# A two-layer decoder segment on one core: second weight chunk in halves, the first norm's squares behind the first weight group, the first group read unscaled, the third group's chunks by parts

## The chip, the core and the metric

The kernel runs on one core of a Trainium2 chip. The metric is the device time of one execution in microseconds (us), as a median of several runs. The engines that matter are TensorE (PE, matrix products), ScalarE (ACT), VectorE (DVE), GpSimd (POOL, nearly idle here) and SyncE (SP), which issues nearly all DMA transfers. Each engine works through its own list of instructions in order; a PE product starts when its operands are there and the product ahead of it has made room.

## What is computed

The program is a decoder segment of two layers over 256 tokens of width 2048: an HGRN2 layer with 16 heads of 128, then a differential-attention layer, each followed by an MLP of width 8192 and a gated embedding. All weights are float32. The change touches only the beginning, the first norm and the first projections of the HGRN2 layer:

```python
def rms_norm(x, gain):
    y = x * rsqrt(mean(x * x, axis=-1) + EPS)
    return y * gain

h = rms_norm(x, ln_mix[0])
q_a, f_a, in_a, g_a = split(h @ a_w_in, 4)        # each (256, 16 heads x 128)
f = lb + (1 - lb) * sigmoid(f_a)                  # forget gate
o = hgrn2_chunkwise(silu(q_a), 1 - f, in_a, log(f))
o = rms_norm(o, a_onorm) * silu(g_a)
x = x + o @ a_w_out
...                                               # MLP, embedding, second layer
```

## The kernel before, in words

Every product of the projections is made in two parts, so that it has float32 accuracy: the weight W is split into a high part hi (a rounding of W) and a low part lo = W - hi, and so is the moving matrix xs. A weight group is 2048 x 512 values (four heads), read as eight chunks of 512 KB (2 x 128 rows by 512 columns) in order. `chunk` (L95 to L101) makes one: a load on SP's queue into `raw` (4 buffers), a cast of `raw` into `hi` on ACT (L99), and a subtraction into `lo` on DVE (L100); `hi` and `lo` have 3 buffers each. `first_chunk` (L103) does the same for the very first chunk in two halves of 256 KB, with its own cast (L113) and subtraction (L114).

`group_b` (L150) makes a group whose output has features on the partitions and tokens along the row. Its products are 128 x 128 of weight against 512 columns (`hi` against both parts of xs, L144) or 256 columns (`lo` against the high part, L147). Per chunk there are 8 pairs of one high and one low product; the sums of a group stay in two PSUM tiles (`mmps`), one for two of the four heads each. With `fresh=2` (group 1 alone) the first two chunks go by `mm_first` (L132, L135): all four heads' products of one half of a chunk before the next half, since xs is also still arriving. With `by_part`, a chunk's high products of a head come before its low ones; without it high and low alternate. The first chunks of the later groups go to the first PSUM tile alone and are caught up later (`for d in ...`), since the second tile may still be read.

At the end of a group `evac` in `project` (L537) reads the sums: for each of the two tiles ACT copies the low half into a buffer `t` (2 buffers, L545), DVE adds the two halves (L547) and, in the kernel before, multiplies by the norm's scale r (`RR[0]`, one value per token) into `z`. So the norm need not be known when the products start: xs is only x times the gain. `start` (L374) loads x transposed (`xa`, 8 pieces), makes xs from it (L200, L201), loads x in rows (`x`, four pieces of 512 KB) and forms the sums of squares of each piece: `square` (L209) writes the squares into a `t` buffer and their sum into `ss`, two ACT operations for each piece. `finish` (L234) then makes r = rsqrt(mean + eps), spreads it over the partitions by a product with a matrix of ones (L244) and copies it (L246).

The order of the groups is: forget gate of heads 0 to 3 (`do_f(0)`, weight group 4), their query (`do_q(0)`, group 0), forget gate of heads 4 to 7 (`do_f(1)`, group 5), their query (`do_q(1)`, group 1), and then the others. After the forget gate, `keys` (L556) turns z into k = 1 - f and G, the running sum of log f: absolute value, exp, log and exp on ACT (`sigmoid_steps`, L276 to L283), four affine operations (L566), a copy (L569), a log (L570), and four scans on DVE (L578, L580). After the query, `silu` does the same four ACT steps and a product on DVE. `hgrn` then computes the recurrence of four heads.

These side computations are Python generators: after each chunk of a group `pump` asks each of them for its next step, so their instructions are written between those of the chunks, and a scheduler orders each engine's list from that. A step written early waits in its engine's list, and whatever stands behind it there waits too. `z` has one buffer in `project` and one in `do_g`.

## Time and profile before

| | |
|---|---|
| median of 3 runs | 2505.16 us (2504.87 to 2505.43) |
| the profiled execution's own time | 2505.13 us |
| its span, first to last instruction in the trace | 2503.3 us |
| PE busy | 2496.0 us (100%) |
| DVE busy | 1544.5 us (62%) |
| ACT busy | 1305.4 us (52%) |
| DMA | 467 MB, 187 GB/s over the span |

The span is what the trace covers; 1.8 us lie around it. Busy time of PE includes products that overlap in its pipeline, so a row's duration in the timeline (0.39 us for a high product) is longer than the step from one product to the next (0.23 us for a high and 0.12 us for a low product). Where PE waited, the next product starts later than that step. Timeline rows of like instructions in a row are put together (x4); their duration is from the first's start to the last's end.

### The profile page before, as it was taken

To read this page: it belongs to the slowest core of one execution; us is meant where nothing else is said; L and a number is where in the kernel's file an instruction comes from. 1 tells how busy PE (TensorE), PEld (TensorE's weight loads), DVE (VectorE), ACT (ScalarE), POOL (GpSimd) and SP (SyncE) were. 2 spreads that over 40 slices of the span, in tenths; PEclk is the share of its full clock that TensorE was granted. 3 is DMA by queue.
4 is the path that set the end of the run, shared out by engine and by line. 5 is a ranking of instruction groups with operands and counts; after the bars stand their busy time and mean duration, and the time that the engine had idled before them with its cause. 6 is when DMAs were issued, how large, how long until landed. Compare 5 with 4: busy or idle time off the path is not lost.

```text
span 2503.3 us, 32238 instructions
## 1 busy us (share of the span) xinstructions
PE 2496.0 (100%) x12552; PEld 2114.3 (84%) x12552; DVE 1544.5 (62%) x1756; ACT 1305.4 (52%) x1669; POOL 6.1 (0%) x12
## 2 busy tenths in 40 slices
PE   9999999999999999999999999999999999999999
PEld 8888888888888888888888888888888888888887
DVE  7887886565565465565576576555556556555565
ACT  8666665444344444444576565544434434444455
POOL 0000000000000000000000000000000000000000
PEclk9999999999999999999999999999999999999999
DMA  7545455556555555555555545555556555555554
GB/s 275 185 152 184 158 172 180 185 186 193 193 188 192 194 192 191 189 193 187 190 179 186 185 151 173 168 185 186 193 189 194 191 193 190 196 192 188 188 201 158
DMA packets 130521, 466.99 MB, mean 187 GB/s; under 512 B 14528, under 2 KB 15168, under 8 KB 130368
## 3 DMA queue, kind: packets, MB, share of 16 engines
q1 hardware_dynamic: 130224, 464.93, 56.2%
q8 instruction: 98, 1.61, 0.3%
q14 instruction: 55, 0.45, 0.1%
q10 hardware_dynamic: 144, 0.01, 0.0%
HBM read 462.78 MB, written 2.10 MB: 186 GB/s over the span
## 4 chain that ended last, share of the span: by engine, by line
PE 99%; DMA 1%; DVE 0%; ACT 0%; SPq 0%; issue 0%
PE mmps L144 23%; PE mmps L175 20%; PE mmps L177 20%; PE mmps L176 20%; PE mmps L147 12%; PE smps L481 1%; PE smps L224 1%; DMA raw<-w_in 0%; DMA x<-x_r 0%; PE smps L512 0%; PE smps L444 0%; PE smps L783 0%; PE smps L819 0%; PE smps L847 0%; PE smps L818 0%; PE smps L530 0%
## 5 line engine op out<-in xcount | busy, mean ns | idle before, releaser
L100 DVE TENSOR_TENSOR lo<-raw,hi 128x1024 fp32r<-128x1024 f32 x869 | 1063.3, 1224 | 870.2 <-ACT hi L99 869.5
L99 ACT CAST hi<-raw 128x1024 fp32r<-128x1024 f32 x869 | 912.6, 1050 | 1045.5 <-PE mmps L177 618.1
L144 PE MATMUL mmps<-big,hi 128*128 128x512 f32 x2544 | 885.7, 395 | 0.0
L175 PE MATMUL mmps<-hi,big 128*128 128x512 f32 x2176 | 853.9, 392 | 0.0
L176 PE MATMUL mmps<-lo,big 128*128 128x512 f32 x2176 | 848.1, 390 | 0.0
L177 PE MATMUL mmps<-hi,big 128*128 128x512 f32 x2176 | 847.8, 390 | 0.0
L147 PE MATMUL mmps<-big,lo 128*128 128x256 f32 x2544 | 703.6, 278 | 0.3 <-DVE lo L100 0.3
L144 PEld LDWEIGHTS mmps<-big,hi 128*128 128x128 f32 x2544 | 476.3, 188 | 108.8
L177 PEld LDWEIGHTS mmps<-hi,big 128*128 128x128 f32 x2176 | 408.4, 188 | 86.0 <-DVE big L122 0.3
L147 PEld LDWEIGHTS mmps<-big,lo 128*128 128x128 f32 x2544 | 478.0, 188 | 3.0 <-DVE lo L100 1.2
L175 PEld LDWEIGHTS mmps<-hi,big 128*128 128x128 f32 x2176 | 408.6, 188 | 82.5
L176 PEld LDWEIGHTS mmps<-lo,big 128*128 128x128 f32 x2176 | 408.8, 188 | 82.1
L298 DVE SCALAR_TENSOR_TENSOR x<-mmps,r,x 128x512 f32<-128x512 f32 x64 | 45.2, 747 | 13.1 <-PE mmps L177 13.1
L200 ACT ACTIVATE big<-smps,sml 128x256 fp32r<-128x256 f32 x96 | 41.0, 471 | 18.0 <-DVE big L201 18.0
L122 DVE TENSOR_TENSOR big<-u,big 128x512 fp32r<-128x512 f32 x72 | 49.3, 685 | 0.0
L201 DVE SCALAR_TENSOR_TENSOR big<-smps,sml,big 128x256 fp32r<-128x256 f32 x96 | 42.2, 479 | 6.6 <-ACT big L200 6.0
L639 DVE SCALAR_TENSOR_TENSOR u<-u 128x512 f32<-128x512 f32 x64 | 44.3, 692 | 2.2
L121 ACT CAST big<-u 128x512 fp32r<-128x512 f32 x72 | 44.4, 616 | 1.9 <-DVE u L639 1.9
L289 ACT COPY t<-mmps 128x512 f32<-128x512 f32 x64 | 37.3, 583 | 14.5 <-PE mmps L147 14.5
L290 DVE TENSOR_TENSOR u<-mmps,t 128x512 f32<-128x512 f32 x64 | 43.8, 684 | 0.0
L212 ACT ACTIVATE t<-x 128x512 f32<-128x512 f32 x48 | 30.3, 631 | 3.9 <-DVE x L669 2.6
L467 ACT ACTIVATE E<-E 128x1024 f32<-128x1024 f32 x16 | 16.9, 1056 | 8.4 <-DVE E L466 8.2
(203 smaller groups left out, 905.2 us busy)
## 6 DMA issues: line engine op xcount, KB each, us to landing
raw<-w_up SPq DMA_DIRECT2D x256, 512.0 KB, 4.2
raw<-w_dn SPq DMA_DIRECT2D x256, 512.0 KB, 3.9
raw<-w_in SPq DMA_DIRECT2D x127, 512.0 KB, 3.3
raw<-w_pg SPq DMA_DIRECT2D x64, 512.0 KB, 3.4
raw<-w_ao SPq DMA_DIRECT2D x32, 512.0 KB, 3.2
raw<-w_k SPq DMA_DIRECT2D x32, 512.0 KB, 3.4
raw<-w_q SPq DMA_DIRECT2D x32, 512.0 KB, 3.3
raw<-w_v SPq DMA_DIRECT2D x32, 512.0 KB, 3.2
```

What stands on the lines that cost most here:

```text
L99: nc.scalar.copy(hi, raw)
L100: nc.vector.tensor_tensor(lo, raw, hi.bitcast(F32), ALU.subtract)
L121: nc.scalar.copy(dst[:, k, 0, :], src)
L122: nc.vector.tensor_tensor(dst[:, k, 1, :], src, dst[:, k, 0, :].bitcast(F32), ALU.subtract)
L144: nc.tensor.matmul(ps[:, ml, :], hi[:, k, w:w + P], rhs[:, k0 + k].rearrange("p a t -> p (a t)"), start=first and k == 0, stop=False)
L147: nc.tensor.matmul(ps[:, ml, T:2 * T], lo[:, k, w:w + P], rhs[:, k0 + k, 0, :], start=False, stop=last and k == KCS - 1)
L175: nc.tensor.matmul(out, xs[:, kc0 + k, 0, ts], hi[:, k], start=st, stop=False)
L176: nc.tensor.matmul(out, xs[:, kc0 + k, 0, ts], lo[:, k], start=False, stop=False)
L177: nc.tensor.matmul(out, xs[:, kc0 + k, 1, ts], hi[:, k], start=False, stop=en)
L290: nc.vector.tensor_tensor(out, ps[:, :, 0:T], t, ALU.add)
L298: nc.vector.scalar_tensor_tensor(xg, ps[:, tt], scale[:, tt, 0:1], xg, ALU.mult, ALU.add)
L639: nc.vector.scalar_tensor_tensor(u, u, 0.0, u, ALU.max, ALU.mult)
```

## The change

There are six edits, all of which act within the first 110 us or so:

- `first_chunk` becomes `fresh_chunk`, used for the first two chunks: chunk 2 of group 1 is now also loaded, cast and subtracted in halves.
- `start` runs over 13 steps in place of 8: the loads of x in rows go out at steps 6 to 9 (before: 4 to 7) and the squares of the four pieces at steps 9 to 12, which is behind group 1. The small constants are loaded one step later, the identity matrix at step 8.
- `finish` has one more step between the diagonal matrices and their product with ones.
- The first group is evacuated unscaled (`project(4 + j, j > 0)`): the sum of the halves is written straight to z. `keys(0)` waits until r is known and then multiplies z by it, in two DVE operations.
- `z` has two buffers in place of one.
- `by_part` is now a number of chunks: all eight for group 5 (the third group), three for group 1 (the fourth); in the MLP it stays at the first chunk.

```diff
@@ -100,19 +100,18 @@
         nc.vector.tensor_tensor(lo, raw, hi.bitcast(F32), ALU.subtract)
         return hi, lo
-    def first_chunk(src):
+    def fresh_chunk(src, c):
         raw = rp.tile([P, KCS, CW], F32, tag="raw", name="raw")
-        hi = wp.tile([P, KCS, CW], F32R, tag="hi", name="hi")
-        lo = wp.tile([P, KCS, CW], F32R, tag="lo", name="lo")
+        hi, lo = (wp.tile([P, KCS, CW], F32R, tag=n, name=n) for n in ("hi", "lo"))
         for k in range(KCS):
             nc.sync.dma_start(raw[:, k], src[:, k * CW:(k + 1) * CW])
-            if k == 0:
+            if c == k == 0:
                 load_xa(0)
         for k in range(KCS):
             nc.scalar.copy(hi[:, k], raw[:, k])
             nc.vector.tensor_tensor(lo[:, k], raw[:, k], hi[:, k].bitcast(F32), ALU.subtract)
-            if k == 0:
+            if c == k == 0:
                 gain_xa(0)
         return hi, lo
@@ -147,18 +146,18 @@
                     nc.tensor.matmul(ps[:, ml, T:2 * T], lo[:, k, w:w + P], rhs[:, k0 + k, 0, :],
                                      start=False, stop=last and k == KCS - 1)
-    def group_b(wsrc, g, rhs, evac, pump=None, fresh=0, by_part=False):
+    def group_b(wsrc, g, rhs, evac, pump=None, fresh=0, by_part=0):
         ps = [mm.tile([P, 2, CW], F32, tag="mm", name="mmps") for _ in range(2)]
         w = []
         for c in range(NCH):
-            w.append((chunk if c or not fresh else first_chunk)(wsrc[g, c]))
+            w.append(fresh_chunk(wsrc[g, c], c) if c < fresh else chunk(wsrc[g, c]))
             if c < fresh:
                 mm_first(ps, *w[c], rhs, c)
             else:
-                mm_b(ps[0], *w[c], rhs, 0, c * KCS, c == 0, c == NCH - 1, by_part and c == 0)
+                mm_b(ps[0], *w[c], rhs, 0, c * KCS, c == 0, c == NCH - 1, c < by_part)
                 for d in ([c] if fresh or c > 1 else [0, 1] if c else []):
                     mm_b(ps[1], *w[d], rhs, 1, d * KCS, d == 0, d == NCH - 1)
             if pump:
@@ -240,6 +239,7 @@
                 dg = ev.tile([P, T], F32, tag="rr", name="dg", bufs=1)
                 for tt in range(2):
                     nc.vector.tensor_scalar(dg[:, tt * P:(tt + 1) * P], ident, rc[:, tt, 0:1], None, ALU.mult)
+                yield
                 ps = sm.tile([P, 512], F32, tag="sm", name="smps")
                 nc.tensor.matmul(ps[:, :T], ones, dg, start=True, stop=True)
                 r = ev.tile([P, T], F32, tag="rn", name="rn", bufs=2)
@@ -373,21 +373,22 @@
     def start():
-        for c in range(8):
+        for c in range(13):
             if c < 7:
                 load_xa(c + 1)
                 gain_xa(c + 1)
-            if c == 3:
+            if c == 4:
                 nc.sync.dma_start(sml, a["small"])
+            if c == 7:
+                bounds()
+            if c == 8:
                 nc.sync.dma_start(ident, a["ident"])
-            if c == 6:
-                bounds()
-            if c > 3:
-                g = c - 4
-                nc.sync.dma_start(x[:, :, g * CW:(g + 1) * CW], a["x_r"][:, :, g * CW:(g + 1) * CW])
-                nrm.square(g)
-            if c < 7:
-                yield
+            if 6 <= c < 10:
+                gs = slice((c - 6) * CW, (c - 5) * CW)
+                nc.sync.dma_start(x[:, :, gs], a["x_r"][:, :, gs])
+            if c > 8:
+                nrm.square(c - 9)
+            yield
         yield from nrm.finish(RR)
         for _ in range(4):
             yield
@@ -534,9 +535,9 @@
                 nc.vector.scalar_tensor_tensor(O[:, m, 1, :], ps, gain, O[:, m, 0, :].bitcast(F32), ALU.mult, ALU.subtract)
                 yield
-        def project(g):
-
-            z = hg.tile(H4, F32, tag="z", name="z", bufs=1)
+        def project(g, scaled=True):
+
+            z = hg.tile(H4, F32, tag="z", name="z")
             def evac(m, ps):
                 m %= 4
@@ -544,18 +545,26 @@
                 t = ev.tile([P, 2, T], F32, tag="t", name="t")
                 nc.scalar.copy(t, ps[:, :, T:2 * T])
                 t, lo = (u.rearrange("p m (c t) -> p m c t", c=2) for u in (t, ps[:, :, 0:T]))
-                nc.vector.tensor_tensor(t, lo, t, ALU.add)
-                nc.vector.tensor_tensor(o, t, bc(RR[0], 2).rearrange("p m (c t) -> p m c t", c=2), ALU.mult)
-
-            group_b(a["w_in"], g, xs, evac, pump, fresh=2 if g == 4 else 0)
+                nc.vector.tensor_tensor(t if scaled else o, lo, t, ALU.add)
+                if scaled:
+                    nc.vector.tensor_tensor(o, t, bc(RR[0], 2).rearrange("p m (c t) -> p m c t", c=2), ALU.mult)
+
+            group_b(a["w_in"], g, xs, evac, pump, fresh=2 if g == 4 else 0, by_part={5: NCH, 1: 3}.get(g, 0))
             return z
         def do_f(j):
-            gens.append(keys(j, project(4 + j)))
+            gens.append(keys(j, project(4 + j, j > 0)))
         def keys(j, z):
             s = st[j]
+            if not j:
+
+                while not RR:
+                    yield
+                for c in range(2):
+                    nc.vector.tensor_tensor(z[:, c], z[:, c], bc(RR[0][:, c * P:(c + 1) * P], 4), ALU.mult)
+                yield
             k = s["k"] = hg.tile(H4, F32, tag="k", name="k")
             G = s["G"] = hg.tile(H4, F32, tag="G", name="G")
             for _ in sigmoid_steps(k, z, G):
@@ -606,7 +615,7 @@
             st[j]["v"] = v
         def do_g(j):
-            z = hg.tile([P, 2, CW], F32, tag="z", name="zg", bufs=1)
+            z = hg.tile([P, 2, CW], F32, tag="z", name="zg")
             group_a(a["w_in"], 12 + j, xs, scaled_a(RR, z), pump)
             st[j]["sg"] = hg.tile([P, 2, CW], F32, tag="sg", name="sg", bufs=1)
             gens.append(silu(st[j]["sg"], z))
@@ -640,7 +649,7 @@
                 split(hid, slice(m, m + 2), u)
             for g in range(4):
-                group_b(up, 4 * qd + g, xs, ev_up, pump, by_part=qd > 0 and g == 0)
+                group_b(up, 4 * qd + g, xs, ev_up, pump, by_part=1 if qd and not g else 0)
             if qd == 3:
                 xo, box = moving(out[0]), []
                 nrm = Norm([(xo, out[1])])
```

The edits move instructions on ACT and DVE. In the lists below, the line number is followed by the operation, its output and inputs (a tile's name with a running number that differs between the two kernels) and the shape. First ACT's list where group 1 ends: `hi` casts of group 1's last chunk and group 2's first, the two copies of the evacuation (`t<-mmps`), and the norm. Before:

```order
L99 CAST hi_400<-raw_398 128x1024
L271 ACTIVATE rc_376<-rc_376,epst_90 128x2
L545 COPY t_387<-mmps_127 128x512
L272 ACTIVATE rc_376<-rc_376 128x2
L545 COPY t_391<-mmps_128 128x512
L99 CAST hi_417<-raw_415 128x1024
L99 CAST hi_448<-raw_446 128x1024
```

And in the changed kernel, where `hi_375` is the cast of group 2's first chunk, `hi_391` and `hi_425` those of its second and third:

```order
L99 CAST hi_375<-raw_373 128x1024
L546 COPY t_364<-mmps_127 128x512
L546 COPY t_367<-mmps_128 128x512
L211 ACTIVATE t_420,ss_104<-x_98 128x512
L211 ACTIVATE t_445,ss_104<-x_98 128x512
L99 CAST hi_391<-raw_389 128x1024
L211 ACTIVATE t_420,ss_104<-x_98 128x512
L211 ACTIVATE t_445,ss_104<-x_98 128x512
L211 ACTIVATE t_470,ss_104<-x_98 128x512
L99 CAST hi_425<-raw_423 128x1024
```

The eight squares (L211) now stand behind group 1's copies, two of them ahead of the cast of chunk 2 of group 2 and three more ahead of that of chunk 3.

Second, ACT's list in group 3 (the forget gate of heads 4 to 7). `zt` is the buffer of the query's silu, `q` its result; `G`, `k` and `z_126` belong to keys(0). Before, keys(0) was done in group 2 and the silu alone stood here:

```order
L99 CAST hi_669<-raw_667 128x1024
L436 ACTIVATE Ek_804<-Ek_804 128x512 x2
L276 ACTIVATE zt_630<-z_395 128x1024
L278 ACTIVATE zt_630<-zt_630 128x1024
L99 CAST hi_692<-raw_690 128x1024
L280 ACTIVATE zt_630<-zt_630 128x1024
L99 CAST hi_716<-raw_714 128x1024
L283 ACTIVATE q_612<-zt_630 128x1024
```

In the changed kernel, from the cast of group 3's third chunk (`hi_647`) to those of its fourth (`hi_672`) and fifth (`hi_703`):

```order
L99 CAST hi_647<-raw_645 128x1024
L276 ACTIVATE G_578<-z_126 128x1024
L546 COPY t_584<-mmps_372 128x512
L278 ACTIVATE G_578<-G_578 128x1024
L280 ACTIVATE G_578<-G_578 128x1024
L276 ACTIVATE zt_607<-z_370 128x1024
L99 CAST hi_672<-raw_670 128x1024
L278 ACTIVATE zt_607<-zt_607 128x1024
L283 ACTIVATE k_577<-G_578 128x1024
L280 ACTIVATE zt_607<-zt_607 128x1024
L575 ACTIVATE z_126<-k_577,lb_120,omlb_121 128x2x128 x4
L283 ACTIVATE q_588<-zt_607 128x1024
```

Behind the last of these stands the cast of `hi_703`: the steps of keys(0) and of the silu now lie between the casts of three chunks of this group.

Third, DVE's list in group 4, between the subtractions of its chunks 7 and 8. `E` belongs to the recurrence of the first four heads, `G`, `tot` to keys(1) of the next four. Before:

```order
L100 TENSOR_TENSOR lo_1000<-raw_997,hi_999 128x1024
L466 TENSOR_TENSOR E_1019<-G_413 128x64x8
L100 TENSOR_TENSOR lo_1038<-raw_1035,hi_1037 128x1024
L578 SCALAR_TENSOR_TENSOR G_839<-segm_92,z_613 128x256 x2
L580 SCALAR_TENSOR_TENSOR G_839<-z_613,segm_92 128x256 x2
```

And in the changed kernel:

```order
L100 TENSOR_TENSOR lo_1003<-raw_1000,hi_1002 128x1024
L467 TENSOR_TENSOR E_1022<-G_578 128x64x8
L587 SCALAR_TENSOR_TENSOR G_842<-segm_92,z_589 128x256
L589 SCALAR_TENSOR_TENSOR G_842<-z_589,segm_92 128x256 x2
L486 COPY_PREDICATED accd_609<-masks_95,smps_991 128x64x4 x2
L593 COPY tot_1032<-G_842 128x8
L594 TENSOR_TENSOR tot_1032<-G_842,z_589 128x8
L100 TENSOR_TENSOR lo_1041<-raw_1038,hi_1040 128x1024
```

Three of the four scans and the masked copies have come to stand between the two subtractions.

## Rows read from the trace of the kernel before

**Rows 1.** Windows: us, busy us by engine, PE clock, DMA share, GB/s

```profile
10.00:20.00 10.00, 9.93 (x56) 8.36 (x55) 9.70 (x24) 9.08 (x19) 0.00 (x0) 1.00 1.05 397
200.00:400.00 200.00, 200.00 (x1044) 171.15 (x1043) 157.51 (x194) 126.99 (x152) 0.95 (x1) 1.00 0.52 171
```

**Rows 2.** Timeline of PE (start us, us; idle before), chunks 1 to 4

```profile
...
8.22 0.63 PE L135 MATMUL mmps<-big,lo 128*128 128x256 f32 x4
9.68 1.19 PE L132 MATMUL mmps<-big,hi 128*128 128x512 f32 x4 [0.82 <-ACT hi L99]
10.94 0.74 PE L135 MATMUL mmps<-big,lo 128*128 128x256 f32 x4
11.52 1.09 PE L132 MATMUL mmps<-big,hi 128*128 128x512 f32 x4
12.45 0.63 PE L135 MATMUL mmps<-big,lo 128*128 128x256 f32 x4
12.92 0.63 PE L144 MATMUL mmps<-big,hi 128*128 128x512 f32 x2
13.38 0.28 PE L147 MATMUL mmps<-big,lo 128*128 128x256 f32 x1
...
```

**Rows 3.** Timeline of ACT, the first three chunks of group 1

```profile
3.99 0.62 ACT L113 CAST hi<-raw 128x512 fp32r<-128x512 f32 x1 [1.97 <-DMA raw<-w_in]
...
5.50 0.62 ACT L113 CAST hi<-raw 128x512 fp32r<-128x512 f32 x1
7.04 0.91 ACT L200 ACTIVATE big<-xa,gain 128x256 fp32r<-128x256 f32 x2 [0.92 <-DMA xa<-x_t]
8.58 1.04 ACT L99 CAST hi<-raw 128x1024 fp32r<-128x1024 f32 x1 [0.63 <-DMA raw<-w_in]
...
10.54 1.05 ACT L99 CAST hi<-raw 128x1024 fp32r<-128x1024 f32 x1
...
```

**Rows 4.** Timeline of DVE, the subtraction of chunk 3 of group 1

```profile
...
11.62 1.22 DVE L100 TENSOR_TENSOR lo<-raw,hi 128x1024 fp32r<-128x1024 f32 x1
...
```

**Rows 5.** Timeline of PE, chunk 8 of group 1 to group 2

```profile
...
26.93 0.62 PE L144 MATMUL mmps<-big,hi 128*128 128x512 f32 x2
27.82 0.38 PE L147 MATMUL mmps<-big,lo 128*128 128x256 f32 x1 [0.27 <-DVE lo L100]
...
30.26 0.39 PE L144 MATMUL mmps<-big,hi 128*128 128x512 f32 x1
...
```

**Rows 6.** Timeline of ACT, the same stretch

```profile
...
26.72 0.63 ACT L212 ACTIVATE t<-x 128x512 f32<-128x512 f32 x1 [0.21 <-DMA x<-x_r]
...
27.48 0.63 ACT L212 ACTIVATE t<-x 128x512 f32<-128x512 f32 x1
...
30.46 0.59 ACT L545 COPY t<-mmps 128x512 f32<-128x512 f32 x1 [0.47 <-PE mmps L147]
30.94 2.00 ACT L99 CAST hi<-raw 128x1024 fp32r<-128x1024 f32 x2
...
```

**Rows 7.** Timeline of DVE, the same stretch, and a scan of group 4

```profile
26.54 1.23 DVE L100 TENSOR_TENSOR lo<-raw,hi 128x1024 fp32r<-128x1024 f32 x1 [1.32 <-ACT hi L99]
...
30.71 1.28 DVE L547 TENSOR_TENSOR t<-mmps,t 128x512 f32<-128x512 f32 x2
...
94.32 1.27 DVE L578 TENSOR_TENSOR_SCAN G<-segm,z 128x256 f32<-128x256 f32 x2
...
```

**Rows 8.** Timeline of PE, between chunks 1 and 2 of group 3

```profile
...
54.37 0.40 PE L144 MATMUL mmps<-big,hi 128*128 128x512 f32 x1
54.81 0.39 PE L147 MATMUL mmps<-big,lo 128*128 128x256 f32 x1
...
```

**Rows 9.** Timeline of ACT, part of keys(0) during group 2

```profile
...
42.93 2.08 ACT L566 ACTIVATE z<-k,lb,omlb 128x256 f32<-128x256 f32 x4
44.91 1.04 ACT L99 CAST hi<-raw 128x1024 fp32r<-128x1024 f32 x1
45.85 1.06 ACT L569 ACTIVATE k<-z 128x1024 f32<-128x1024 f32 x1
...
```

## The prediction

> **What bounds the kernel now.** I read the busy times by stretch first, then the timelines of TensorE (PE), ScalarE (ACT) and VectorE (DVE) over the first 110 us. From 200 to 400 us PE is busy for all 200.00 us; from 10 to 20 us it is not quite [rows 1]. So an edit of the work on ACT, on DVE or in the queue is worth something only where it removes a wait of PE, and the reader should look for those. All that exceed 0.1 us lie in the first 55 us, at three places.
>
> First, weight chunk 2 of the first group. Four high-part products take 0.93 and four low-part ones 0.47 (11.52, 12.45, 12.92), so 0.23 and 0.12 each. The low ones that start at 8.22 are through at 8.70, but chunk 2's products start at 9.68; its first low part comes at 10.94 in place of 10.71 [rows 2]. The cause is the cast of the whole chunk, from 8.58, when the load lands, to 9.62 [rows 3]. Second, chunk 8 of that group: its first two products start at 26.93, the low part at 27.82 in place of 27.39, because the subtraction runs from 26.54 to 27.77 [rows 5, 7]. Third, 0.2 us at the third group's second chunk: 54.81 in place of 54.60 [rows 8]. The product after a wait is also 0.1 late (those at 10.94 and 27.82 show 0.1 more than their like). Together some 2.3 us: this is all that can be won.
>
> The sum is made against the profiled execution, 2505.13 us with its span of 2503.3; the median of the three runs is 2505.16, so the change is added to it as it is. Chunks are counted from 1 in each group; group 1 is the forget gate of the first four heads, 2 their query, 3 and 4 the same for the next four.
>
> **Part 1, chunk 2 in halves.** Removed: one load of 512 KB, one cast of 1.04, one subtraction of about 1.22. Added: two of each at half size. A half cast takes 0.62 [rows 3]; for a half subtraction I take half of 1.22 [rows 4] and 0.1. The loads of that stretch run at 397 GB/s with the DMA engines full [rows 1], so 256 KB take 0.66 and the whole chunk lands when it did. ACT is free at 7.95 (7.04 and 0.91); the first half lands between 7.04 and 8.58, one half's time before the end most likely, 7.9. So its cast ends near 8.57 and PE goes on at 8.70 without a wait. The second half is cast from 8.58 to 9.20. PE needs 2 x (0.93 + 0.47) = 2.8, so chunk 2 is done at 11.5 and not at 12.92. But chunk 3 is not there: its cast starts with its load at 10.54 and ends at 11.59 [rows 3], its subtraction runs from 11.62 to 12.84 [rows 4], and its low part starts at 12.89 where it stood at 13.38 [rows 2]. So 1.4 us are gained and 0.9 of it lost to the next chunk: **-0.49**.
>
> The extra issue on SP costs PE nothing: the loads behind it queue at full DMA engines. The Trainium skill speaks against this edit ("DMA: Bandwidth & Descriptors", Rules for kernel authors): make transfers of 1 MiB or more and gather small ones. Its section Anatomy of one DMA prices each at about 2.0 us and its bytes over 436 GB/s; halves served in turn would by that add an estimated 2.0. The trace does not bear this out: the two halves of chunk 1 are cast at 3.99 and 5.50 with another load between them [rows 3]. I take no cost; the case is among the rivals.
>
> **Part 2, the squares and x go later.** The four loads of x (512 KB, 1.3 us each) now stand behind weight chunks 7 to 10, and the eight squares behind group 1. Three such loads stood ahead of chunk 8; now one does, so it lands some 2.6 us earlier and its cast finds ACT free. The wait of 0.43 and the 0.1 behind it go: **-0.53**. Group 2 starts at 30.26 [rows 5] - 0.49 - 0.53 = 29.24.
>
> Here the moved squares collide, and this is the first new cost. ACT's order at the start of group 2 is now: copy, copy, square, square, cast of chunk 2, three squares, cast of chunk 3. Before, the cast stood right behind the copy, 30.46 to 30.94 [rows 6]. The second copy waits for group 1's last product: from 29.44 (0.2 after the turn of the groups, as 30.46 stands to 30.26) to 30.03. DVE adds it until 30.75 (0.69 [rows 7]). The first square starts at 29.92; the second writes the t buffer that DVE reads until 30.75, so it starts at 30.78; the cast follows at 31.5 (0.63 and its read of the sum) and ends at 32.55. PE has 8 pairs of products for chunk 1 at 0.35, 2.8, and wants chunk 2 at 32.0: wait **0.6**. The subtraction runs from 32.6 to 33.83; PE wants it two products after the cast, at 33.06: wait **0.8**. Then three squares (0.76 each, 26.72 to 27.48 [rows 6]) put the cast of chunk 3 at 34.75 to 35.8 and its subtraction's end at 37.05, wanted at 36.7: **0.35**. With 0.1 behind each: **+2.05**. The other squares stand one ahead of each cast and hide. Chunk 4 then starts at 39.5 and group 3 at 39.5 + 5 x 2.8 + 0.2 (the ones product) = 53.7; 2.8 is (26.93 - 12.92) / 5 [rows 2, 5].
>
> **Part 3, group 3.** The scale z x r leaves group 1's evacuation and becomes two DVE operations of about 0.68 in keys(0) as group 2 ends, where DVE has room. By-part order swaps products of the same cost and lets a chunk's low part come 0.23 later. It, and the DVE work that is now elsewhere, remove the wait at 54.81: **-0.31** with the 0.1 behind it.
>
> But keys(0) waits for the norm, now done in group 2, and so its chain on ACT moves from beside group 2 to group 3, where silu of the query already is. An activation of 1024 elements costs 0.94 to the next, or its 1.06 if the next reads it; the four affine ones 1.98 [rows 9]. From 53.8, when group 2's last cast buffer comes free, ACT does: cast of chunk 3, absolute value, copy, exp, log, absolute value, cast of chunk 4, exp, exp, log, four affine, exp, and only then the cast of chunk 5. The steps before it sum to 9 x 0.94 + 0.48 + 1.06 + 1.98 = 12.0, so it runs from 65.8 to 66.9, and PE wants it at 53.7 + 4 x 2.8 = 64.9: wait **2.0**. On DVE the q x z product (1.22) stands before the subtraction: 66.0 to 67.2, then until 68.4; PE wants it after three high products, 67.6: **0.8**. With 0.1 behind each: **+3.0**. Chunks 6 to 8 get a cast every 1.9 us against PE's 2.8 and hide.
>
> **Part 4, group 4.** On DVE, between the subtractions of chunks 7 and 8, there now stand half a difference, three scans of 0.6 [rows 7], two masked copies and two small ones, over 4 us with the subtraction itself, against 2.8 of PE; PE would wait 0 to 1.5 for chunk 8, by how early that of chunk 7 was. Below nothing is excluded, since PE has no wait there now. I take the middle, **+0.9** with the 0.1 behind. Later the order is as before but for a shift, and PE has no wait there to win or lose: 0.
>
> Sum: -0.49 - 0.53 - 0.31 + 2.05 + 3.0 + 0.9 = +4.6; 2505.13 + 4.6 = **2509.7 us**, slower by 0.18%.
>
> **Rivals.** A: the change does what its parts offer and the new waits stay away, because the casts in groups 2 and 3 keep ahead of PE. Then -1.3 remains: 2503.8. For it: ACT is busy for 9.08 of 10 us at the start and for 127 of 200 later [rows 1], so there is room on average. Against it: the queue is in order, and the cast of chunk 5 has 12.0 us of ACT's work ahead of it in 11.2 us of PE's. B, slower than the forecast's bound: what piled up in group 3 is not drained there. PE then waits in groups 3 and 4 for every chunk whose subtraction ends over 0.5 us (two products) after its cast's first use; from four such chunks at 0.6 on it counts: +2.4, 2512.1. For it: DVE has over 4 us of other work between two subtractions of group 4. Against: a cast every 1.9 us catches up within three chunks. C, half of the new waits: squares and chain each hide by half of their 5.05: 2507.2. D: the halves are not served back to back, and the second lands with the next load, 10.54 in place of 8.58 [rows 3]: the loads behind it are 1.96 late, and chunk 3's low part with them: 2511.7. This is what the skill's rule above comes to.
>
> **How the numbers follow.** Forecast 0.66, A 0.08, B 0.12, C 0.11, D 0.03. The range, 2506.8 to 2511.2, holds the forecast with the unknown costs of parts 2 to 4, and C; A, D and B's centre are left out. A measurement of this kernel can tell about 0.2%, 5.0 us, from no change: the bounds are 2500.2 and 2510.2. The forecast lies 0.5 below the upper one, so a quarter of its 0.66 counts as slower, with B and D: 0.32. Faster needs -5.0, and only 2.3 can be won: 0.01. The rest, 0.67, is within.
>
> **What would show it.** In the profile after: products of chunk 2 of group 1 from 8.7 and the low part of chunk 3 at 12.9 (part 1). Group 2 from 29.2, and PE idle for 0.6 and 0.8 at 32 to 34 with squares ahead of the late cast (part 2). PE idle for 2 us at 65 to 67, released by the cast, with the affine operations just ahead of it on ACT (part 3). About 0.8 near 102, released by a subtraction (part 4). No wait near 67 would make the forecast wrong by 3 us, towards C; waits at every chunk of group 4 would make it B.

## The result, and the profile after

The changed kernel takes 2509.89 us (median of 19 runs, 2508.45 to 2511.45) against 2505.20 us for the kernel before (19 runs); the ratio is 1.0018, 95% interval 1.0012 to 1.0024. The forecast was 2509.7 us. The total was met, but not every term of it: the waits came to 1 us less than forecast, and something that the forecast did not have, a slower TensorE clock behind one of them, made up for it.

The profiled execution has a span of 2508.0 us, 4.7 us more than before. Main products of the same number in both traces give where it came from: the table takes the time from one high product to another, from the two PE timelines. A chunk has 8 pairs of products; in group 3 the first 8 pairs are half of chunk 1's and half of chunk 2's, so that row is named by its pairs.

| stretch | before, us | after, us | difference | forecast |
|---|---|---|---|---|
| to the start of group 2 | 30.26 | 29.39 | -0.87 | -1.02 |
| group 2 | 22.73 | 24.29 | +1.56 | +2.05 |
| group 3, first 8 pairs | 3.10 | 2.78 | -0.32 | -0.31 |
| group 3, the other 56 pairs | 19.68 | 23.56 | +3.88 | +3.0 |
| group 4 | 25.04 | 25.56 | +0.52 | +0.9 |
| the rest | 2402.5 | 2402.4 | -0.1 | 0 |

**Group 1.** PE's timeline of the changed kernel, chunks 2 and 3 (columns: start in us, us, engine, line, operation, output and inputs; in brackets the idle time ahead and what ended it), answers to [rows 2]:

```profile
8.93 1.09 PE L131 MATMUL mmps<-big,hi 128*128 128x512 f32 x4
...
11.77 0.73 PE L143 MATMUL mmps<-big,hi 128*128 128x512 f32 x2
13.03 0.38 PE L146 MATMUL mmps<-big,lo 128*128 128x256 f32 x1 [0.53 <-DVE lo L100]
...
15.48 0.39 PE L143 MATMUL mmps<-big,hi 128*128 128x512 f32 x1
...
29.39 0.40 PE L143 MATMUL mmps<-big,hi 128*128 128x512 f32 x1
...
```

The last two rows are the first products of chunk 4 and of group 2; PE has no wait between them. Chunk 2's products run without a wait from 8.93 (8.7 was forecast, but here the kernel's first product is 0.24 us later than before, at 6.03), and chunk 3 starts at 11.77 in place of 12.92, but its low part comes at 13.03, where 12.9 was forecast. The halves are cast back to back as they land, and the next load is 0.1 us later than the 10.54 of [rows 3]. ACT's timeline:

```profile
8.06 1.28 ACT L112 CAST hi<-raw 128x512 fp32r<-128x512 f32 x2
...
10.67 1.05 ACT L99 CAST hi<-raw 128x1024 fp32r<-128x1024 f32 x1 [0.34 <-DMA raw<-w_in]
...
```

**Group 2.** The timelines of PE, ACT and DVE at its second chunk, in that order, answer to [rows 5 to 7]:

```profile
32.65 0.73 PE L143 MATMUL mmps<-big,hi 128*128 128x512 f32 x2 [0.27 <-ACT hi L99]
33.91 0.39 PE L146 MATMUL mmps<-big,lo 128*128 128x256 f32 x1 [0.53 <-DVE lo L100]
```

```profile
30.07 0.64 ACT L211 ACTIVATE t<-x 128x512 f32<-128x512 f32 x1
...
30.93 0.63 ACT L211 ACTIVATE t<-x 128x512 f32<-128x512 f32 x1
...
31.57 1.03 ACT L99 CAST hi<-raw 128x1024 fp32r<-128x1024 f32 x1
...
```

```profile
30.21 0.69 DVE L548 TENSOR_TENSOR z<-mmps,t 128x512 f32<-128x512 f32 x1 [0.49 <-ACT t L546]
32.63 1.23 DVE L100 TENSOR_TENSOR lo<-raw,hi 128x1024 fp32r<-128x1024 f32 x1 [1.73 <-ACT hi L99]
...
```

The second square starts at 30.93, when DVE has read the `t` buffer (30.21 and 0.69), the cast stands behind it until 32.60, and PE, whose last product of chunk 1 starts at 32.10, goes on at 32.65. It is the chain that the forecast described, 0.07 us off.

**Group 3.** PE's timeline from the last product of chunk 4, then ACT's and DVE's:

```profile
64.68 0.27 PE L146 MATMUL mmps<-big,lo 128*128 128x256 f32 x1
66.93 1.50 PE L143 MATMUL mmps<-big,hi 128*128 128x512 f32 x3 [1.98 <-ACT hi L99]
68.39 0.79 PE L146 MATMUL mmps<-big,lo 128*128 128x256 f32 x2
68.98 1.05 PE L143 MATMUL mmps<-big,hi 128*128 128x512 f32 x2
69.83 0.84 PE L146 MATMUL mmps<-big,lo 128*128 128x256 f32 x3
...
71.57 0.63 PE L143 MATMUL mmps<-big,hi 128*128 128x512 f32 x2
...
```

```profile
62.93 2.06 ACT L575 ACTIVATE z<-k,lb,omlb 128x256 f32<-128x256 f32 x4
64.90 1.04 ACT L283 ACTIVATE q<-zt 128x1024 f32<-128x1024 f32 x1
65.85 1.03 ACT L99 CAST hi<-raw 128x1024 fp32r<-128x1024 f32 x1
...
```

```profile
65.97 1.23 DVE L604 TENSOR_TENSOR q<-q,z 128x1024 f32<-128x1024 f32 x1 [1.69 <-ACT q L283]
67.12 1.22 DVE L100 TENSOR_TENSOR lo<-raw,hi 128x1024 fp32r<-128x1024 f32 x1
...
```

The cast of chunk 5 runs from 65.85, behind the four affine operations and the silu's exp, as forecast; PE waits 2.0 us. What follows was not forecast: three high products take 1.50 us in place of 0.85, and two alike go from 0.62 to 1.05. The windows say why (columns as in [rows 1]; the number ahead of the last two is the granted clock):

```profile
60.00:65.00 5.00, 4.95 (x29) 4.07 (x28) 2.45 (x2) 5.00 (x9) 0.00 (x0) 1.00 0.31 107
...
67.00:68.00 1.00, 1.00 (x3) 0.61 (x3) 1.00 (x2) 1.00 (x2) 0.00 (x0) 0.56 0.00 0
68.00:69.00 1.00, 1.00 (x5) 0.61 (x4) 0.53 (x2) 1.00 (x2) 0.00 (x0) 0.50 0.00 0
69.00:70.00 1.00, 1.00 (x4) 0.81 (x4) 1.00 (x2) 1.00 (x2) 0.00 (x0) 0.50 0.68 135
70.00:71.00 1.00, 1.00 (x7) 0.95 (x6) 1.00 (x3) 0.67 (x1) 0.00 (x0) 0.73 0.90 348
...
```

One of these windows in the kernel before:

```profile
68.00:69.00 1.00, 1.00 (x8) 0.86 (x7) 1.00 (x2) 0.42 (x1) 0.00 (x0) 1.00 0.77 299
```

The reader is to see that PE is busy all through 67 to 70 us and yet has only 3 to 5 products in each window, at a granted clock of 0.50 (0.56 in the first), which is 1.2 GHz in place of 2.4; in the kernel before the three windows have a clock of 1.00 and 7 or 8 products. Up to the low product at 68.39 this costs nothing, since that one waits for the subtraction, which ends at 68.34 (67.12 and 1.22). From there to the first product of chunk 6, at 71.57, are 3.18 us. At full clock a chunk takes 2.77 us and three high products of it 0.69, so the rest is 2.08 and the clock takes 1.1.

**Group 4.** One wait, at the place forecast, released by the subtraction with the three scans and the masked copies ahead of it on DVE. PE's and DVE's timelines:

```profile
102.91 0.39 PE L146 MATMUL mmps<-big,lo 128*128 128x256 f32 x1 [0.31 <-DVE lo L100]
```

```profile
99.07 0.68 DVE L587 TENSOR_TENSOR_SCAN G<-segm,z 128x256 f32<-128x256 f32 x1
99.67 1.25 DVE L589 TENSOR_TENSOR_SCAN G<-z,segm 128x256 f32<-128x256 f32 x2
100.84 0.74 DVE L486 COPY_PREDICATED accd<-masks,smps 128x256 f32<-128x256 uint8 x2
...
101.64 1.22 DVE L100 TENSOR_TENSOR lo<-raw,hi 128x1024 fp32r<-128x1024 f32 x1
...
```

### The profile page after: what moved, and what is told of

Its sections match the earlier page's. It is cut to its first block, busy times and chain, and to the rows that moved or that the text cites. A ratio compares the mean times of both kernels' runs of the same rounds, so it can differ in the third digit from the quotient of the medians.

```text
span 2508.0 us, 32243 instructions
## 1 busy us (share of the span) xinstructions
PE 2498.2 (100%) x12552; PEld 2116.0 (84%) x12552; DVE 1544.3 (62%) x1757; ACT 1305.1 (52%) x1670; POOL 6.6 (0%) x12
## 4 chain that ended last, share of the span: by engine, by line
PE 98%; ACT 1%; DVE 1%; DMA 0%; issue 0%; SPq 0%
PE mmps L143 23%; PE mmps L176 20%; PE mmps L174 20%; PE mmps L175 20%; PE mmps L146 11%; PE smps L223 1%; PE smps L482 1%; PE smps L513 0%; PE smps L792 0%; PE smps L828 0%; PE smps L856 0%; DMA raw<-w_in 0%; ACT hi L99 0%; PE smps L445 0%; DVE lo L100 0%
## 5 line engine op out<-in xcount | busy, mean ns | idle before, releaser
L211 ACT ACTIVATE t<-x 128x512 f32<-128x512 f32 x48 | 30.2, 629 | 3.5 <-DVE x L678 2.6
```

## The experiments

Differences of less than some 2 us are read from the chunk starts in the profiles, since the medians' intervals are about 0.1% (2.5 us) wide on either side.

**Part 1 alone, and the change without it.** The first is the kernel before with the new `fresh_chunk`; the second is the changed kernel with

```diff
-            w.append(fresh_chunk(wsrc[g, c], c) if c < fresh else chunk(wsrc[g, c]))
+            w.append(fresh_chunk(wsrc[g, c], c) if c < min(fresh, 1) else chunk(wsrc[g, c]))
```

Part 1 alone:

> The kernel before with part 1 alone: chunk 2 of the first group is loaded, cast and subtracted in halves. Theory: PE goes on with chunk 2 without a wait, chunk 3's low part is 0.5 us earlier than before relative to the first product, and the lead stays to the end: 2505.2 - 0.5 = 2504.7 us. Rival D of the prediction (halves cost queue time): the low part of chunk 3 is about 2 us later, 2506.7 us or more.

The change without part 1:

> The changed kernel without part 1 (chunk 2 of the first group whole again), everything else as changed. Theory: the 0.5 us at the start are lost again and all later waits stay as they are: 2509.9 + 0.4 to 0.5 = 2510.3 us. Rival: the new waits in groups 2 and 3 end at times that the start doesn't move (loads), and so take the 0.5 us up: 2509.9 us.

Measured: part 1 alone 2505.98 us against 2505.53 beside it, ratio 1.0002 (0.9993 to 1.0011); the change without it 2509.52 us, 1.0015 (1.0006 to 1.0024). Neither median can tell the times that were expected apart, since they differ by less than the intervals; in the profiles part 1 is worth nothing that shows. PE's waits with part 1 alone:

```profile
9.00 1.20 PE L131 MATMUL mmps<-big,hi 128*128 128x512 f32 x4 [0.47 <-DVE big L200]
13.11 0.39 PE L146 MATMUL mmps<-big,lo 128*128 128x256 f32 x1 [0.53 <-DVE lo L100]
27.88 0.39 PE L146 MATMUL mmps<-big,lo 128*128 128x256 f32 x1 [0.27 <-DVE lo L100]
```

The low part of chunk 3 waits for its load, cast and subtraction, at 13.11. Chunk 4 then starts between 15.30 and 15.75 in eight profiles with part 1 (those with chunk 3 in halves too are left out), and at 15.39, 15.71 and 15.82 in three without it: the loads' own spread is as large as the term. The first product of chunk 4 in the kernel before:

```profile
15.71 0.39 PE L144 MATMUL mmps<-big,hi 128*128 128x512 f32 x1
```

And in the kernel before a lead there is lost again at chunk 8, whose load comes behind three loads of x: its low part starts at 27.88 with part 1 alone and at 27.82 without [rows 5], and group 2 at 30.34 and 30.26. The change without part 1 starts group 2 at 29.30, the whole change at 29.39, so the lead of 0.9 us there doesn't need part 1. From chunk 4 to group 2 both take 13.91 us, where the kernel before takes 14.55: these 0.64 us are what part 2 brings. The rest is where chunk 4 starts, which differs from profile to profile as said.

**Chunk 3 in halves too.** The kernel before with part 1, `fresh=3` and half casts for chunk 3, half casts for chunk 2 of group 3 and order by parts for its first two chunks.

> The kernel before with part 1, and also chunk 3 of the first group cast and subtracted in halves (loaded whole), its products half by half; chunk 2 of the third group cast in halves and by parts. The norm stays where it was. Theory: the wait that part 1 moved to chunk 3's low part goes, about 0.9 us more than with part 1 alone at chunk 4, of which later chunks (bound by their loads) take back some 0.6; the 0.3 us at the third group go: 2505.2 - 0.5 - 0.3 - 0.3 = 2504.1 us. Rival: the extra instructions on ACT and DVE, which are over 90% busy there, eat it: 2504.7 us or more.

Measured: 2504.86 us, ratio 0.9996 (0.9987 to 1.0005), which can't be told from no change. The profile tells more. The first products of chunks 4 and 8 in PE's timeline:

```profile
14.14 0.63 PE L146 MATMUL mmps<-big,hi 128*128 128x512 f32 x2
...
26.95 0.63 PE L146 MATMUL mmps<-big,hi 128*128 128x512 f32 x2
```

Chunk 4 is 1.57 us earlier than before, chunk 7 0.87, and chunk 8 starts as before (26.93 [rows 5]). Here all of the lead is taken back by the loads, not 0.6 of it as expected. The 0.3 us at group 3 are won: its first 8 pairs take 2.79 us in place of 3.10.

**The squares one at a time, with earlier loads.**

```diff
...
-            if 6 <= c < 10:
+            if 4 <= c < 8:
...
-            if c > 8:
-                nrm.square(c - 9)
+            if 5 <= c:
+                nrm.square((c - 5) // 2, ((c - 5) % 2,))
```

The lines at the first `...` give `square` its second argument.

> The changed kernel with the loads of x two chunks earlier and the eight squares one at a time behind eight chunks (6 to 13) in place of two at a time behind four, so that the last one stands where it stood and keys(0) with it. Theory (the squares ahead of the cast of chunk 2 of group 2 cause its waits of 0.43 and 0.69 us): of these 1.3 us about 0.4 is left, while the 2 us wait in group 3 stays: about 2509.0 us. Rival (the loads set these waits): they stay, 2509.9 us.

Measured: 2510.19 us, 1.0018 (1.0009 to 1.0027). The median can't tell 2509.0 from 2509.9, and the profile shows neither theory. Group 2 takes 23.25 us in place of 24.29, without a wait over 0.3; but the loads of x, two chunks earlier, are back ahead of chunks 7 and 8:

```profile
24.79 0.39 PE L146 MATMUL mmps<-big,lo 128*128 128x256 f32 x1 [0.49 <-DVE lo L100]
28.10 0.39 PE L146 MATMUL mmps<-big,lo 128*128 128x256 f32 x1 [0.26 <-DVE lo L100]
```

Group 2 starts at 30.55, 1.16 us later than with the change. One wait was exchanged for the other, and so it does not separate squares from loads. The next run does.

**Short squares.** The squares are taken over 64 of each 512 columns; this leaves out seven eighths of the first norm's sum and nothing else.

```diff
-                nc.scalar.activation(flat(t), x[:, tt, g * CW:(g + 1) * CW], AF.Square, accum_out=self.ss[:, tt, g:g + 1])
+                w = CW // 8 if self.row else CW
+                nc.scalar.activation(flat(t)[:, :w], x[:, tt, g * CW:g * CW + w], AF.Square, accum_out=self.ss[:, tt, g:g + 1])
```

> The changed kernel with the squares of the first norm taken over 64 of each 512 columns, so that each costs ACT some 0.3 us in place of 0.76 (this leaves out seven eighths of the first norm's sum and so changes its scale; loads, casts and all other steps are there). The norm is then ready some chunks earlier, and keys(0) stands in group 2 as it did before the change. Theory (the time is lost because 6 us of squares and then keys(0) are put where ACT's list has no room): of the waits of 1.3 us in group 2 some 0.8 is left (a little at the cast, 0.7 at the subtraction), those of 3.9 us in group 3 and 0.6 in group 4 go, and the clock stays at full speed: about 2505 us, level with the kernel before. Rival (what costs is that x itself comes later, or the two new DVE operations): 2508 us or more.

Measured: 2504.48 us (10 runs), 0.9996 (0.9986 to 1.0006), clock 1.000. Between 30 and 110 us PE has one wait left:

```profile
33.68 0.39 PE L146 MATMUL mmps<-big,lo 128*128 128x256 f32 x1 [0.53 <-DVE lo L100]
```

The loads of x are as late as in the change, and so are the first group's unscaled z and the two new DVE operations. Without the squares' time on ACT, keys(0) is back in group 2, and 5.4 us are gone. So the loss comes from the squares' time where they were put in ACT's list, directly and through keys(0), which has to wait for the norm behind them.

**The silu three chunks later.** One edit in the changed kernel: `silu` of the first query yields three times before its first step.

> The changed kernel with the first query's silu begun three chunks later, so that its four steps on ACT no longer stand among those of keys(0). Theory (the two chains together stand ahead of the cast of chunk 5 of group 3): no wait of 2 us near 65 us and no half-speed clock behind it; two waits of 0.7 to 0.9 us come in chunks 6 and 7 in its place, from the silu's steps; those in group 2 and the 0.5 us of group 4 stay: 2509.9 - 3.9 + 1.8 = 2507.8 us. Rival (keys(0) alone is too long for the room in group 3): a wait of over 1 us stays at chunk 5 and the time within 0.5 us of 2509.9.

Measured: 2508.27 us, 1.0010 (1.0001 to 1.0019). Chunk 5 of group 3 has no wait. Two shorter ones have come between 71 and 74 us, and the one in group 4 is longer than expected:

```profile
71.94 0.49 PE L143 MATMUL mmps<-big,hi 128*128 128x512 f32 x1 [0.42 <-ACT hi L99]
73.22 0.51 PE L146 MATMUL mmps<-big,lo 128*128 128x256 f32 x2 [0.78 <-DVE lo L100]
102.27 0.39 PE L146 MATMUL mmps<-big,lo 128*128 128x256 f32 x1 [0.91 <-DVE lo L100]
```

The clock stays at 1.00 behind them:

```profile
68.00:72.00 4.00, 3.58 (x20) 2.63 (x19) 4.00 (x9) 3.91 (x6) 0.00 (x0) 1.00 0.38 131
72.00:76.00 4.00, 3.22 (x17) 2.60 (x18) 4.00 (x7) 1.53 (x2) 0.00 (x0) 1.00 0.39 141
```

From 0.6 us behind the kernel before at chunk 5, the lag grows only to some 2.5 at the end of group 3, where the change lags by 4.25. The two chains together, not keys(0) alone, made the wait of 2 us.

**No order by parts.**

> The changed kernel without by-part order in the third and fourth group. Theory of the prediction (the order by parts and the DVE work that went elsewhere together remove the 0.3 us at chunk 2 of group 3): 0.2 to 0.3 us come back there, and the low product of chunk 5 is wanted earlier, so PE idles there once more: about 2510.3 us. Rival (the DVE work alone removes it): the start of group 3 stays as with the change, 2509.9 us.

Measured: 2510.55 us, 1.0020 (1.0011 to 1.0029). The first 8 pairs of group 3 take 2.77 us, as with the change and not 3.10 as before: the DVE work that went elsewhere removes the 0.3 us alone, and the order by parts isn't needed for it. (It isn't the only way: half casts and order by parts won the same in the kernel before, as seen above, where DVE's work stayed.) At chunk 5 the low product is wanted earlier and PE idles 0.73 us once more; from there to chunk 6 are 5.17 us in place of 4.64. The wait of group 4 is gone in this run: that group takes 25.13 us, with the change 25.56 and before 25.04. Its first three chunks have lost the order by parts, and PE comes to it 0.66 us later; no run tells which of the two does it.

**Both collisions taken apart.** Loads two chunks earlier, squares one at a time and one chunk earlier, and the silu three chunks later.

> The changed kernel with both collisions taken apart: loads of x two chunks earlier, squares one at a time and done one chunk earlier, and the first query's silu three chunks later. Theory: of the waits of 1.3 us in group 2 about 0.4 is left, of the 3.9 us in group 3 about 1, the clock stays at full speed, and group 4 has no wait: level with the kernel before, 2505.2 to 2505.8 us. Rival (deferring the norm costs by itself, wherever its work stands): 2508 us or more.

Measured: 2506.70 us, 1.0005 (0.9996 to 1.0013); the clock is 1.000. It is between the two expectations: 1.1 us behind the kernel before, measured beside it, where the change is 4.7 behind. Group 2 starts 0.6 us late (chunks 7 and 8 wait for their loads again), and one wait of 0.8 us is left in group 3.

**The squares on GpSimd.** The products x * x go to GpSimd, which is idle, and their sums to reductions on DVE. The first version is the change with this alone; the second adds chunk 3 in halves, squares right behind the loads, scans in two steps and the silu two chunks later.

> The changed kernel with the first norm's squares made as products on GpSimd (idle there) and their sums as reductions on DVE, at the same places of the program; ACT's list keeps its order but for the eight squares, which are gone from it. Theory (the squares on ACT ahead of the cast cause the waits of 0.43 and 0.69 us in group 2): these go, while the wait of 2 us in group 3 and the half-speed clock behind it stay: 2509.9 - 1.3 = 2508.6 us. Rival (those waits come from the later loads): they stay, 2509.9 us. GpSimd's time for a product is not shown by any trace so far; if it is over 2.7 us, the norm comes later and keys(0) with it.

> A version with the change's gains and without its waits: chunks 2 and 3 of the first group in halves, x loaded behind chunks 7 to 10 as in the change, its squares on GpSimd with sums on DVE as soon as each piece is there, the scans of the keys in two steps, the first query's silu two chunks later. Theory: the lead of 0.9 us at the end of group 1 and the 0.3 us at group 3 stay, one wait of some 0.4 us comes in group 3: 2505.2 - 0.8 = 2504.4 us. Rival (GpSimd's products slow DVE or come late): 2505.2 us or more.

Measured: 2512.05 us, 1.0028 (1.0017 to 1.0038), and 2508.60 us, 1.0014 (1.0005 to 1.0023). Both theories missed; the rival of the second came out. GpSimd and DVE at the start of group 2, in the first version:

```profile
28.67 1.04 POOL L213 TENSOR_TENSOR t<-x 128x512 f32<-128x512 f32 x1 [0.80 <-DVE ss L214]
30.51 1.95 POOL L213 TENSOR_TENSOR t<-x 128x512 f32<-128x512 f32 x1 [0.80 <-DVE ss L214]
```

```profile
29.74 0.69 DVE L214 TENSOR_REDUCE ss<-t 128x1 f32<-128x512 f32 x1 [1.15 <-POOL t L213]
30.35 1.22 DVE L100 TENSOR_TENSOR lo<-raw,hi 128x1024 fp32r<-128x1024 f32 x1
...
```

DVE stands idle for 1.15 us before the reduction, because this waits for GpSimd, and the subtraction that PE needs is queued behind it; PE idles 1.75 us until 31.62, and again 1.43 us until 39.13; the wait of 2 us in group 3 stays. The second version has the first two waits as well (1.75 us until 31.88, 1.41 until 39.39). So a free engine for the squares didn't help here: the reductions stand in DVE's list ahead of a weight chunk's subtraction, as the squares stood in ACT's ahead of a cast. (The profile's spans on GpSimd are rough.)

**Pauses.** The kernel before with one chunk's cast repeated in 15 groups of the first MLP, so that PE idles there.

```diff
...
-        nc.scalar.copy(hi, raw)
+        for _ in range(1 + int(again)):
+            nc.scalar.copy(hi, raw)
+        if again % 1:
+            nc.scalar.copy(hi[:, 0], raw[:, 0])
...
```

The rest of the edit hands `again` to the fifth chunk of each of these groups and puts its chunks from there on in order by parts.

> The kernel before with the cast of the fifth chunk repeated 3.5 to 6 times in 15 weight groups of the first MLP (by parts there from the fifth chunk on), so that PE idles there for about 0.4, 0.9, 2.3, 2.7 or 3.8 us, several times each, with steady products before and after. It measures what the clock does after an idle stretch. If an idle stretch of 2 us is what halves the clock at 67 us in the changed kernel, then the granted clock behind the stretches of 2.3 us and more is near 0.5 for some 3 us in most of them, and stays at 1.00 behind those of 0.4 and 0.9 us. If the fall belongs to the place, group 3 with its other work, the clock stays at 1.00 behind all of them.

Measured: 2559.3 us (2 runs), with a mean clock of 0.995. Windows behind an idle stretch of 0.60 us (the first line), behind two of 2.06 us (the second and the last) and behind the one of 2.51 us that left the clock up (the third):

```profile
555.40:559.40 4.00, 3.70 (x19) 2.90 (x20) 3.44 (x3) 1.33 (x2) 0.00 (x0) 1.00 0.39 138
580.84:582.84 2.00, 2.00 (x6) 1.56 (x7) 2.00 (x2) 0.00 (x0) 0.00 (x0) 0.51 0.00 0
694.44:696.44 2.00, 1.71 (x7) 1.18 (x8) 2.00 (x2) 0.00 (x0) 0.00 (x0) 1.00 0.00 0
922.50:924.50 2.00, 2.00 (x8) 1.78 (x7) 1.49 (x2) 0.00 (x0) 0.00 (x0) 0.50 0.76 264
```

The clock stayed at 1.00 behind the three stretches of 0.60 us, and fell to 0.50 behind eight of the nine longer ones (2.06 us four times, 2.5 three times, 3.6 twice), at once or within 2 us, for some 3 us. So the fall is not a matter of group 3; it follows an idle stretch of PE of about the length that the change makes there, most times and not always. The profiles agree: all five with the wait in group 3 (the change, and those without part 1, with single squares, without parts and with GpSimd) idle there for 1.91 to 2.00 us and show the fall behind it, while the four waits of 1.41 to 1.75 us in the two GpSimd versions left the clock at 1.00. The window behind the one that ended at 31.62:

```profile
31.62:34.62 3.00, 3.00 (x17) 2.63 (x18) 2.87 (x4) 0.80 (x2) 2.03 (x2) 1.00 0.54 175
```

The changed kernel's 19 runs fall in two sets: in 7 the clock averages 1.000 and the median is 2508.6 us; the other 12 are the slowest, average 0.999 or less (one of them 0.949) and have a median of 2510.2. That the 12 had the fall and the 7 had none is argued from this and not shown run by run, since an average of 0.999 also occurs without the wait, in 6 of 33 runs of the kernel before. By these medians the fall costs 1.6 us, by the one profile 1.1.

## Why the prediction was right, step by step

**What held.** That little can be won in the first 55 us (2.3 us at most by the working; -0.87 and -0.32 came), and that ACT's list order in groups 2 and 3 loses more than that. Group 2's two waits were at 32.65 and 33.91, where 32.6 and 33.83 stood in the working; the cast of chunk 5 started at 65.85 (65.8), group 3 at 53.67 (53.7). Rivals A and C fell with that. B fell too: chunks 6 to 8 of group 3 had no wait. D fell: the halves landed within 0.7 us of one another, and chunk 3 was 0.1 us later, not 1.96. The fixed price of a transfer (the Trainium skill, "DMA: Bandwidth & Descriptors", Anatomy of one DMA) did not show here as time of the queue; the section gives it for transfers that GpSimd issues, and these are issued by SP.

**Part 1, mis-sized.** The step "1.4 us are gained and 0.9 of it lost to the next chunk: -0.49" took the cast of chunk 3 as fixed at 10.54 and put its low part at 12.89. In the profiles that cast starts between 10.5 and 10.9, as its load lands, and the low part came at 13.03. Chunk 4 starts 0.23 us earlier than before in the profile of the change, and over all profiles the starts with it and without overlap. In the kernel before a lead there is worth nothing in any case, since the load of chunk 8 takes it back; only with part 2, which brings that load forward, can it reach group 2. Part 2's own term was a little small: -0.53, where 0.64 us were saved between chunk 4 and group 2. The two errors nearly cancel, -1.02 against -0.87.

**Group 2, mis-sized.** Two of three waits came, 0.43 and 0.69 in place of 0.6 and 0.8; the third, 0.35 at chunk 3, did not. Three squares were put at 0.76 each, the step from 26.72 to 27.48 of [rows 6]; back to back they took 0.62 each (32.50, 33.12, 33.74), so the subtraction there was done at 36.64, and it was wanted at 36.80. What the two waits and the 0.1 behind each don't account for in the +1.56 is that pairs of products took 0.353 us in place of 0.347 (chunks 3 to 6 of the group: 11.29 us, before 11.09); no run shows why. +1.56 in place of +2.05.

**Group 3, right but for what follows a wait.** The two waits took 2.13 us (64.80 to 66.93) and 0.67 (at full clock the three high products, 0.69 and 0.1 behind the wait, would be through at 67.72, and the low one came at 68.39), where 2.0 and 0.8 were forecast: the cast was on time to 0.1 us, the subtraction too (68.34, forecast 68.4). What the step lacked is the clock, 1.1 us in the profile: nothing in the trace of before shows PE idle for 2 us, and so nothing shows what follows it. In the seven runs whose clock averages 1.000 the kernel takes 2508.6 us, 1.1 below the forecast; that the median lies on the forecast is luck: the waits were put 1 us too high, and the fall, which the forecast doesn't have, brings as much. The range held both.

**Group 3's first wait.** -0.32 as forecast, but the cause was half wrong: the order by parts isn't needed for it.

**Group 4.** Place and releaser were right; the middle of the range, +0.9, was too much: +0.52, of which the wait for the subtraction is 0.47 (102.44 to 102.91).

## What to carry to other kernels

An engine with half its time free still has no room in the one stretch where its list is full: before moving work to "later", add up what stands in its list between two instructions that the bottleneck needs, and compare with the time that the bottleneck gives. A gain ahead of a place that waits for a load is taken back there: 1.57 us at chunk 4 were none at chunk 8. And a wait of some 2 us on TensorE should be priced with the slow clock behind it: 1.1 us for a wait of 2.1 here.

## What the runs showed of the hardware

The granted clock of TensorE fell to half behind 8 of 9 idle stretches of 2.06 to 3.58 us that were made for this, and behind all five waits of 1.91 to 2.00 us in the profiles; it stayed behind one of 2.51 us, four of 1.41 to 1.75 and three of 0.60. The products behind a fall take twice as long for some 3 us (two high ones 0.85 us from 68.98 to 69.83, in place of 0.46). The Trainium skill tells in "TensorE: Matmul & The Clock Gate" (HAM oscillation) that a wait between stretches of products can put the clock back; the trace agrees.

A product of a 128x512 tile with itself on GpSimd takes 1.04 us while DVE is idle and 1.95 us when it starts beside a DVE subtraction of two tiles (30.51 beside 30.35 above); the eight average 1.50 us. The Trainium skill says in "SBUF — State Buffer" (Who interferes with whom) that a DVE operation with two inputs in SBUF contends with a GpSimd one that reads SBUF; the trace agrees. It goes the other way too. In the same run this small DVE operation, with one tile as input, started 0.04 us behind a GpSimd product of 1.04 us (from 24.08) and took 1.03 us, ending with it, where in the changed kernel it takes 0.17 (23.03):

```profile
24.12 1.03 DVE L361 TENSOR_SCALAR omlb<-lb 128x16 f32<-128x16 f32 x1
```
